# A planner that books busy intervals, earlier memory loads, and mLSTM scores from split float32r parts

## The chip, the cores and the metric

The kernel runs on one core of one Trainium2 chip. The metric is the device time of one execution in microseconds (us), the median of several runs. Engines are named as in the profile: PE multiplies matrices (PEld loads its weights), DVE is the vector engine, ACT the scalar engine, POOL the third elementwise engine, SP and POOL also issue transfers (DMA).

## The reference

The kernel computes a trunk of two layers on 512 tokens of width 1024, all in float32, with a memory of 256 rows. Cut to what matters:

```python
# layer 0: x += fox_diff_mixer(rms_norm(x)); x += cross_attention(x, mem); x += conv_ffn(x)
# layer 1: x += mlstm_mixer(rms_norm(x));    x += cross_attention(x, mem); x += conv_ffn(x)
# out = rms_norm(x)
def fox_diff_mixer(xn, ...):           # 8 forgetting heads (fq, fk, fv), 4 differential heads (dq, dk, dv)
    p = softmax(q @ k.T * scale + F_q - F_k)            # forgetting: decays F from a gate
    p = softmax(q1 @ k1.T * scale) - lam * softmax(q2 @ k2.T * scale)   # differential
    d_out = rms_norm(p @ v, subln) * (1 - lambda_init)  # a norm per head
    return concat(fox_out, d_out) @ w_out
def mlstm_chunkwise(q, k, v, i_pre, log_f):             # 4 heads; q, k after a causal convolution and silu
    scores = (q @ k.T) * W                              # W: exp of gate sums, masked
    num = scores @ v
    den = maximum(abs(scores.sum(-1)), exp(-m))
    h = num / den                                       # then a norm per head, an output gate, and @ w_out
```

## The kernel before

Everything is written transposed where PE needs it, in tiles of 128 partitions. Most products are "split": a float32 value is kept as a high part (a cast to float32r) and a low part (the rest, also float32r), and `mm3` (lines 340 to 342 before, 373 to 375 after) issues three float32r products: high x high, low x high, high x low. Weights come by SP into one of three `raw` buffers of 128 x 1024; ACT casts them to `wh`, DVE subtracts to `wl` (line 262 in the profile is the helper that records all DVE and ACT operations; it is line 295 after). The products gather in four accumulator banks `acc`, in two banks `s` and two banks `w` of PSUM.

Layer 0's mixer runs over heads. The differential heads come first: projections dv, dq, dk; q and k are rotated into `qa`, `ka`, `kb`; a score row (lines 750, 751; 783, 784 after) of up to 512 columns is reduced with its mask or decay on DVE into `x` and `sm`; the scaled row is turned (line 781; 814) by transposes through a `w` bank into `pt`; the weigh (lines 793 and 1008; 826 and 1041) multiplies `pt` with v. Each differential head and the first three mLSTM heads end in a "far norm" (`p_far_norm`): sums of squares on PE (line 499; 532), `z` on DVE, a power on POOL, the roots written to memory and read back spread over all partitions as `hrb` (lines 448 and 452; 481 and 485, both issued by POOL), and a DVE step that multiplies by them. The first stretches of the next weights' work (`p_fill`: the memory's keys `xk`, and the output projection `wo`) fill PE where the mixer itself has none.

Layer 1's mixer projects values (`mv`, token major), queries and keys (`mqk`) and output gates (`mog`). `conv` makes q and k; the gates' columns come by small transposes (line 1630; 1663). Per head come four scores, one for each block of 128 keys with 512, 384, 256 and 128 queries (line 1721), multiplied by a mask tile `mk` into `at`; the denominators (lines 1743, 1744; 1781 after) sum the four `at` with a matrix of ones; the numerators (line 1765; 1802) multiply `at` with v.

The order within the mixers and attentions is set by a planner, class `Plan`. Its items have a length on PE, dependencies, a priority, banks and buffers they take and free, and a chain of steps on ACT ("A"), DVE ("D"), POOL ("G") or waiting ("-") that follows. Where several are ready the lowest priority number goes first. Before, each engine is one number, the time from which it is free:

```python
            for e, d in pick.chain:
                u = max(u, eng[e]) + d
                eng[e] = u
```

The instructions are issued in the order in which items are picked, and on the chip each engine runs its own in that order. The FFN has another planner, class `Sched`.

Of the kernel before, what the change touches and what calls it, by code (L numbers as in the profile page):

```python
# [30 lines left out]
ROW_DMA, SPREAD_DMA, LATE = 2.7, 6.0, 12.0  # L31
# [51 lines left out]

class Plan:
# [3 lines left out]
    def __init__(self, prev=None, hold=(), **res):  # L88
        self.items = []
        self.t = prev.t if prev else 0.0  # L90
        self.eng = dict(prev.eng) if prev else {"A": 0.0, "D": 0.0, "G": 0.0}
        self.res = {k: [0.0] * n for k, n in res.items()}
        self.banks = {b: 0.0 for b in range(4) if b not in hold}
        self.res["acc"] = self.banks.values()

    def add(self, fn, dur=0.0, deps=(), prio=None, take=(), free=(), chain=(), pre=(), after=0.0, order=(), load=(), st=None):
        it = Item(fn, dur, [d for d in deps if d is not None], len(self.items) if prio is None else prio, take, free, chain, pre, after, order, load, st)
        it.n = len(self.items)
        self.items.append(it)
        return it  # L100

    def run(self):
        todo = sorted(self.items, key=lambda i: (i.prio, i.n))
        eng, t = self.eng, self.t
        while todo:
            soon, pick = float("inf"), None
            held = set()
            for i in todo:
                if any(d.ready is None for d in i.deps + i.order) or held & set(i.take):
                    continue  # L110
                held |= set(i.take)
                if any(len(self.res[r]) < i.take.count(r) for r in i.take):
                    continue
                at = max([i.after] + [d.ready for d in i.deps] + [sorted(self.res[r])[i.take.count(r) - 1] for r in i.take])
# [8 lines left out]
            todo.remove(pick)  # L123
            for r in pick.take:
                if r == "acc":
                    b = min(self.banks, key=self.banks.get)
                    del self.banks[b]
                    pick.st.setdefault("banks", []).append(b)
                else:
                    self.res[r].remove(min(self.res[r]))  # L130
            for e, d in pick.pre:
                eng[e] = max(eng[e], t - 4.0) + d
            t += pick.dur
            u = t + (0.1 if pick.chain else 0.0)
            for e, d in pick.chain:
                if e == "-":
                    u += d
                    continue
                u = max(u, eng[e]) + d
                eng[e] = u  # L140
                u += 0.06
            for e, d in pick.load:
                eng[e] = max(eng[e], t) + d
            pick.ready = u
            pick.fn()
            for r in pick.free:
                if r == "acc":
                    self.banks[pick.st["banks"].pop(0)] = u
                else:
                    self.res[r].append(u)  # L150
        self.t = t
        return t
# [136 lines left out]
class Builder:  # L289
# [64 lines left out]
    def p_proj(self, pl, src, xs, evac, chain, deps=(), kdeps=None, edeps=(), prio=None, n=SEQ, nk=KB8, order=None, etake=(), per=2, eorder=(), load=()):  # L354
# [5 lines left out]
        for c, e in zip(cuts, cuts[1:] + [nk]):  # L360
# [12 lines left out]
            for k in ks:  # L373
# [4 lines left out]
                pre=(("A", 0.12 * nk), ("D", 0.14 * nk)) if first else (), st=st,  # L378
# [1607 lines left out]
```

## Time and profile before

| what | value |
|---|---|
| median of 3 runs | 1425.7 us (1424.77 to 1426.21) |
| profiled execution, its own time | 1423.48 us |
| its span | 1421.7 us |
| mean granted PE clock | 0.998 |
| PE busy | 1403.3 us, 99% |
| DVE, ACT, POOL busy | 80%, 58%, 9% |
| layer 0: mixer, output projection and attention, FFN | 0 to 225, to 330, to 725 us |
| layer 1: mixer, output projection and attention, FFN | to 890, to 1090, to 1415 us |

The span runs from the first to the last instruction of the profiled execution; 1.8 us lie around it. Busy shares are averages over these stages. In rows of instructions, lines are those of the kernel before; a tile's name stands ahead of `<-`, its inputs behind.

### The profile page before, as it was taken

What the parts mean: (1) busy time and instruction counts of PE and PEld (TensorE: products, weight loads), DVE (VectorE), ACT (ScalarE), POOL (GpSimd) and SP (SyncE); (2) the same over time, 40 slices, a digit from 0 to 9 for tenths busy, and PEclk for the clock granted to TensorE, in tenths of its full rate; (3) what the DMA queues carried; (4) which work ended last, traced back from release to release, by engine and by line L of the source; (5) the groups of instructions that cost most, each with busy time, mean ns of one, the idle gap of its engine ahead of it and who ended that gap; (6) DMA issues with size and microseconds to landing.
All of it is one profiled execution on the core that took longest, in us unless ns stands there. A gap on an engine that the chain in (4) does not pass through costs nothing.

```text
span 1421.7 us, 22241 instructions
## 1 busy us (share of the span) xinstructions
PE 1403.3 (99%) x8440; PEld 1262.9 (89%) x8440; DVE 1133.5 (80%) x1906; ACT 823.8 (58%) x1382; POOL 129.9 (9%) x189
## 2 busy tenths in 40 slices
PE   9999999999999999999999999999999999999998
PEld 7878788899889999999887788989988999999997
DVE  7778596666689999999768657667667999999984
ACT  7777574444476656566456654445445665656655
POOL 0001240000001111110001210000000111111000
PEclk9999999999999999999999999999999999999999
DMA  5233224323248777773233322323323886777522
GB/s 205 90 108 108 90 79 152 132 76 133 86 150 217 191 180 184 182 182 106 86 105 112 105 95 97 119 92 120 130 74 120 212 202 171 193 179 185 143 77 80
DMA packets 69211, 190.02 MB, mean 134 GB/s; under 512 B 7552, under 2 KB 7552, under 8 KB 69104
## 3 DMA queue, kind: packets, MB, share of 16 engines
q1 hardware_dynamic: 55648, 153.48, 32.3%
q0 software_dynamic: 12448, 34.00, 13.7%
q8 instruction: 66, 1.08, 0.3%
q10 hardware_dynamic: 1008, 1.12, 0.2%
q14 instruction: 41, 0.34, 0.1%
HBM read 186.43 MB, written 2.15 MB: 133 GB/s over the span
## 4 chain that ended last, share of the span: by engine, by line
PE 83%; DVE 8%; ACT 4%; issue 3%; DMA 1%; POOL 1%; SPq 0%; POOLq 0%; DVEq 0%; ACTq 0%
PE acc L340 16%; PE acc L341 16%; PE acc L342 16%; PE w L340 5%; PE w L342 5%; PE w L341 5%; PE s L340 3%; PE s L341 3%; PE s L342 3%; PE acc L402 2%; PE acc L404 2%; PE acc L403 2%; DVE wl L262 2%; DVE x L262 1%; PE w L1765 1%
## 5 line engine op out<-in xcount | busy, mean ns | idle before, releaser
L262 ACT CAST wh<-raw 128x1024 fp32r<-128x1024 f32 (+2 forms) x229 | 235.0, 1027 | 205.6 <-PE acc L341 118.8
L262 DVE TENSOR_TENSOR wl<-raw,wh 128x1024 fp32r<-128x1024 f32 (+2 forms) x229 | 274.2, 1198 | 38.7 <-ACT wh L262 38.2
L340 PE MATMUL acc<-xh,wh 128*128 128x512 f32 (+1 forms) x800 | 278.6, 348 | 0.8 <-ACT v L262 0.8
L341 PE MATMUL acc<-xl,wh 128*128 128x512 f32 (+1 forms) x800 | 274.0, 343 | 0.0
L342 PE MATMUL acc<-xh,wl 128*128 128x512 f32 (+1 forms) x800 | 273.6, 342 | 0.0
L340 PEld LDWEIGHTS acc<-xh,wh 128*128 128x128 f32 x800 | 152.5, 191 | 14.5 <-ACT v L262 1.2
L342 PEld LDWEIGHTS acc<-xh,wl 128*128 128x128 f32 x800 | 152.4, 190 | 13.9
L341 PEld LDWEIGHTS acc<-xl,wh 128*128 128x128 f32 x800 | 152.5, 191 | 13.2
L262 DVE SCALAR_TENSOR_TENSOR c<-hs,vec,c 128x512 f32<-128x512 f32 x176 | 131.8, 749 | 3.8 <-ACT c L262 0.8
L340 PE MATMUL w<-ah,wh 128*128 128x512 f32 x304 | 115.7, 381 | 0.2 <-ACT c L262 0.2
L342 PE MATMUL w<-ah,wl 128*128 128x512 f32 x304 | 115.2, 379 | 0.0
L341 PE MATMUL w<-al,wh 128*128 128x512 f32 x304 | 115.2, 379 | 0.0
L262 ACT ACTIVATE c<-hs,vec 128x512 f32<-128x512 f32 x88 | 70.8, 811 | 9.9 <-DVE hs L262 5.4
L262 ACT CAST ah<-c 128x512 fp32r<-128x512 f32 x44 | 27.2, 619 | 83.8 <-DVE c L262 83.8
L262 DVE TENSOR_TENSOR x<-acc,x 128x512 f32<-128x512 f32 (+1 forms) x43 | 28.1, 653 | 54.2 <-PE acc L342 53.4
L340 PEld LDWEIGHTS w<-ah,wh 128*128 128x128 f32 x304 | 57.6, 190 | 8.0 <-DVE x L262 0.9
L342 PEld LDWEIGHTS w<-ah,wl 128*128 128x128 f32 x304 | 57.5, 189 | 8.1
L341 PEld LDWEIGHTS w<-al,wh 128*128 128x128 f32 x304 | 57.6, 190 | 6.5
L342 PE MATMUL acc<-mem,wl 128*128 128x256 f32 (+1 forms) x192 | 59.9, 312 | 0.0
L340 PE MATMUL acc<-mem,wh 128*128 128x256 f32 (+1 forms) x192 | 59.6, 311 | 0.0
L341 PE MATMUL acc<-mem,wh 128*128 128x256 f32 (+1 forms) x192 | 59.6, 311 | 0.0
L1446 POOL DMA_DIRECT2D sa<-in_up_dram x36 | 30.8, 857 | 290.6 <-DMA sa<-in_up_dram 212.7
(357 smaller groups left out, 3750.5 us busy)
## 6 DMA issues: line engine op xcount, KB each, us to landing
raw<-in_up_dram SPq DMA_DIRECT2D x52, 512.0 KB, 3.7
sa<-in_up_dram SPq DMA_DIRECT2D x36, 512.0 KB, 3.4
sa<-in_up_dram POOLq DMA_DIRECT2D x36, 512.0 KB, 5.9
raw<-in_down_dram SPq DMA_DIRECT2D x32, 512.0 KB, 3.6
ra<-in_up_dram SPq DMA_DIRECT2D x36, 256.0 KB, 4.0
sb<-in_up_dram POOLq DMA_DIRECT2D x36, 256.0 KB, 4.9
raw<-in_xk_dram SPq DMA_DIRECT2D x16, 512.0 KB, 3.2
raw<-in_wo_dram SPq DMA_DIRECT2D x16, 512.0 KB, 3.3
```

What stands on the lines that cost most here:

```text
L262: i = issue(*a, **k)
L340: mm(out, wh, xh, start=first, stop=False, skip_group_check=parts)
L341: mm(out, wh, xl, start=False, stop=False, skip_group_check=parts)
L342: mm(out, wl, xh, start=False, stop=last, skip_group_check=parts)
L402: mm(ps, xh[k][:, ts], wh, start=(k == 0), stop=False)
L403: mm(ps, xh[k][:, ts], wl, start=False, stop=False)
L404: mm(ps, xl[k][:, ts], wh, start=False, stop=(k == 7))
L1446: return add("POOL", 0.0029 * cols, lambda: nc.gpsimd.dma_start(out(), src(), accum_op=ALU.add), deps, due, (), (), 6.0)
L1765: nc.tensor.matmul(ps[:, lo:], vv[s][:, c], a[:], start=(s == 0), stop=(s == 3))
```

## The change

The planner. An engine is now a list of busy intervals, and a step goes into the first gap that holds it (`place`). An item that is ready only later than 2.5 us from now (`HOLD`) no longer keeps its banks from items of lower priority. The plan is first made as a whole (`ordered`) and then issued. A projection's accumulator bank counts as free after the first step of its chain (`soon`). Costs of steps are changed (a cast 0.5 to 0.6, the roots on POOL 1.05 to 1.3, the far norm's round trip `LATE` 12 to 15). Memory loads are issued 16 us ahead of their use instead of 10. In layer 1 the gates' chain is one wait of 14 us with its load beside it.

The mLSTM. q and k are kept as high and low parts (one more DVE step each), and a score is an `mm3` instead of one float32 product. The denominators' sum is completed by a copy, split by a cast on ACT and a subtraction on DVE, and multiplied with ones in two float32r products of 512 columns, instead of float32 products of 128 and 384. The sum uses a tile of tag `th` instead of `mk`. In all PE's rows go from 8101 to 8133, DVE's from 1809 to 1825, ACT's from 1275 to 1278; POOL and SP keep theirs.

```diff
-ROW_DMA, SPREAD_DMA, LATE = 2.7, 6.0, 12.0
+ROW_DMA, SPREAD_DMA, LATE = 2.7, 6.0, 15.0
...
+HOLD = 2.5
...
-        self.eng = dict(prev.eng) if prev else {"A": 0.0, "D": 0.0, "G": 0.0}
+        self.eng = prev.eng if prev else {"A": [], "D": [], "G": []}
...
+        def place(e, at, d):
+            b = eng[e]
+            while b and b[0][1] < t - 8.0:
+                b.pop(0)
+            n = 0
+            for n, (x, y) in enumerate(b):
+                if at + d <= x:
+                    break
+                at = max(at, y)
+            else:
+                n = len(b)
+            b.insert(n, (at, at + d))
+            return at + d
...
-                held |= set(i.take)
-                if any(len(self.res[r]) < i.take.count(r) for r in i.take):
+                if any(len(res[r]) < i.take.count(r) for r in i.take):
+                    held |= set(i.take)
                     continue
...
+                if at < t + HOLD:
+                    held |= set(i.take)
...
             for e, d in pick.pre:
-                eng[e] = max(eng[e], t - 4.0) + d
+                place(e, t - 4.0, d)
...
             for e, d in pick.chain:
-                if e == "-":
-                    u += d
-                    continue
-                u = max(u, eng[e]) + d
-                eng[e] = u
-                u += 0.06
+                u = u + d if e == "-" else place(e, u, d) + 0.1
+                clear = clear or u
...
-            last = pl.add(lambda c=c: load(c), 0, (), 0, after=at + step * c - 10.0, order=[*order, last])
+            last = pl.add(lambda c=c: load(c), 0, (), 0, after=at + step * c - 16.0, order=[*order, last])
...
-            g = pl.add(lambda: None, 0, [g], 1, chain=(("A", 1.0), ("D", 7.0), ("A", 0.5)))
-            gk = pl.add(lambda: None, 0, [g], 2, chain=(("-", ROW_DMA),))
+            g = pl.add(lambda: None, 0, [g], 1, chain=(("-", 14.0),), load=(("A", 5.0), ("D", 7.0)))
+            gk = pl.add(lambda: None, 0, [g], 2, chain=(("-", 4.0),), load=(("A", 2.4), ("D", 1.2)))
...
-                out = self.til(mp, tag, bufs=2)
-                nc.scalar.activation(out[:], c[:], AF.Copy, scale=scale)
-                return out
+                hi, lo = (self.til(mp, tag + i, dtype=F32R)[:] for i in ("", "l"))
+                nc.scalar.activation(hi, c[:], AF.Copy, scale=scale)
+                nc.vector.scalar_tensor_tensor(out=lo, in0=c[:], scalar=scale, in1=hi.bitcast(F32), op0=ALU.mult, op1=ALU.subtract)
+                return hi, lo
...
-                        nc.tensor.matmul(ps[:, :n], st["k"][:, ks], st["q"][:, lo:512], start=True, stop=True)
+                        (kh, kl), (qh, ql) = st["k"], st["q"]
+                        self.mm3(ps[:, :n], kh[:, ks], kl[:, ks], qh[:, lo:], ql[:, lo:], True, True)
...
-                    asum = st["sum"] = self.til(mp, "mk")
+                    asum = st["sum"] = self.til(mp, "th")
...
+                    nc.vector.tensor_copy(asum[:, :P], at[0][0][:, :P])
+                    st["d"] = [self.til(mp, "mk", dtype=F32R)[:] for _ in range(2)]
+                    self.split(*st["d"], asum[:])
...
-                    nc.tensor.matmul(den[:, :P], self.ones[:], st["at"][0][0][:, :P], start=True, stop=True)
-                    nc.tensor.matmul(den[:, P:], self.ones[:], asum[:, P:], start=True, stop=True)
+                    for i, part in enumerate(st["d"]):
+                        nc.tensor.matmul(banked(den[:]), self.onesr[:], alternate(part), start=i == 0, stop=i == 1)
```

More of the change, by code (lines that the diff above doesn't have):

```diff
@@ L377, in p_proj, with p_proj_tok @@
                 fn, 3 * len(ks) * MM * n / 512, d, prio, take=("acc", "wt") if first else (), free=("wt",) if e == nk else (),
[L378 removed]
+                pre=(("A", 0.13 * nk), ("D", 0.14 * nk)) if first else (), st=st,
             )
[L380 to L382 removed]
+        return pl.add(lambda: evac(st["ps"]), 0, [last, *edeps], prio, take=etake, free=("acc",), chain=chain, order=eorder, load=load, st=st, soon=True)
+    def p_proj_tok(self, pl, src, xs, ntok, evac, deps=(), kdeps=None, edeps=(), prio=None, n=512, etake=(), ready=None, rest=True):
         st = {}
```

129 lines of the change are left out of this document (71 added, 58 removed).

## The prediction

> **What bounds the kernel now.** First the page: busy shares and the chain that ended last.
>
> ```profile
> span 1421.7 us, 22241 instructions
> PE 1403.3 (99%) x8440; PEld 1262.9 (89%) x8440; DVE 1133.5 (80%) x1906; ACT 823.8 (58%) x1382; POOL 129.9 (9%) x189
> PE 83%; DVE 8%; ACT 4%; issue 3%; DMA 1%; POOL 1%; SPq 0%; POOLq 0%; DVEq 0%; ACTq 0%
> ```
>
> PE is the bound, so the time changes in two ways only: PE gets less work, or waits less. Next the stages, in the windows view (columns: window, its length, busy us of PE, PEld, DVE, ACT and POOL, granted clock, DMA share, GB/s).
>
> ```profile
> 20.00:150.00 130.00, 127.37 (x633) 109.18 (x632) 99.94 (x260) 99.00 (x198) 12.42 (x19) 1.00 0.32 104
> 150.00:156.00 6.00, 3.50 (x22) 3.18 (x21) 3.85 (x12) 2.40 (x7) 3.23 (x5) 0.94 0.33 87
> 156.00:160.00 4.00, 4.00 (x13) 3.23 (x13) 2.58 (x5) 2.64 (x6) 1.96 (x4) 0.66 0.24 66
> 180.00:210.00 30.00, 28.55 (x208) 24.39 (x208) 28.80 (x102) 22.91 (x59) 12.03 (x22) 1.00 0.19 63
> 330.00:725.00 395.00, 394.84 (x2602) 366.76 (x2602) 347.54 (x512) 229.67 (x368) 33.64 (x42) 1.00 0.56 152
> 725.00:890.00 165.00, 161.43 (x739) 133.44 (x738) 112.68 (x172) 91.41 (x134) 24.17 (x41) 1.00 0.31 101
> ```
>
> Layer 0's mixer ends near 225; after the attention the FFN fills 330 to 725, and layer 1's mixer, the mLSTM, ends near 890. The FFN is full, and the change doesn't touch it. What can be won lies in the two mixers. The waits view puts a few names on it (who waits, for whom; us in total, times, longest).
>
> ```profile
> PE w L781 <- DVE pt L262: 2.5, 1, 2.5
> PE s L1721 <- ACT k L262: 1.8, 2, 0.9
> PE s L1630 <- DVE cv L262: 1.5, 1, 1.5
> PE w L793 <- ACT pt L262: 1.0, 1, 1.0
> PE w L781 <- DVE sm L262: 0.9, 1, 0.9
> ```
>
> Records of matmuls overlap (0.38 us long, 0.22 apart), so their idle time understates what is lost. I therefore count work from start to start. These rows give the steps (start, length):
>
> ```profile
> 198.97 0.33 PE L751 MATMUL s<-kb,qa 128*128 128x384 f32 x1
> 199.13 0.38 PE L750 MATMUL s<-ka,qa 128*128 128x512 f32 x1
> 199.34 0.38 PE L751 MATMUL s<-kb,qa 128*128 128x512 f32 x1
> ...
> 162.50 0.27 PE L750 MATMUL s<-ka,qa 128*128 128x256 f32 x1
> 162.61 0.28 PE L751 MATMUL s<-kb,qa 128*128 128x256 f32 x1
> ...
> 787.94 0.38 PE L1743 MATMUL w<-at,ones 128*128 128x128 f32 x2
> 788.16 0.81 PE L1744 MATMUL w<-mk,ones 128*128 128x384 f32 x2
> 788.81 0.82 PE L1721 MATMUL s<-q,k 128*128 128x256 f32 x4
> ...
> 160.88 0.49 PE L781 MATMUL w<-ident,x 128*128 128x128 f32 x3
> 161.12 0.46 PE L340 MATMUL acc<-xh,wh 128*128 128x512 f32 x1
> ```
>
> A float32r product takes 0.16 us for 384 columns, 0.21 to 0.22 for 512, 0.11 for 256. A plain float32 one (recorded as two) takes 0.22 for 128 and 0.65 for 384: 1.7 ns a column. Three transposes take 0.24. With these steps, 180 to 210 holds 23.7 us of work and loses 6.3, at a DVE that is busy 28.8 of 30 us; 160 to 225 loses 9.1 in all, 20 to 150 6.1, 725 to 890 4.8.
>
> **The products.** Per head the mLSTM's scores are four float32 products of 512, 384, 256 and 128 columns, 1280 x 1.7 = 2.17 us, and the denominators 512 columns, 0.87. After: scores 3 x (0.22 + 0.16 + 0.11 + x), denominators two float32r products of 512, 0.44. x, a float32r product of 128 columns, is not in the trace. Between 0.08 (a transpose of 128 columns above) and 0.22 (float32) I take 0.11, the nearest row of that type. A head saves 3.04 - 1.80 - 0.44 = 0.80, four heads **3.2 us** (1.9 to 3.6). By the Trainium skill, TensorE: Matmul & The Clock Gate, section "Wait — 56ns, not 53.3ns?", x would be 0.056 on a warm array; the saving would be estimated at 3.8.
>
> On DVE this adds eight low parts, four subtractions and four copies; on ACT four casts. From the groups by line (busy us, mean ns; then idle time before and its releasers), the nearest operations:
>
> ```profile
> L262 DVE SCALAR_TENSOR_TENSOR cv<-hs,vec,cv 128x512 f32<-128x512 f32 x24 | 18.3, 763 | 0.3
> L262 DVE COPY pt<-w 128x128 f32<-128x128 f32 x24 | 6.9, 286 | 2.1 <-ACT pt L262 1.7 <-PE w L781 0.2
> L262 DVE COPY pt<-w 128x384 f32<-128x384 f32 x12 | 6.5, 548 | 0.9 <-PE w L781 0.9
> ```
>
> That is 8 x 0.76, four subtractions at no more than that and 4 x 0.29, some 10 us on a DVE busy 112.7 of 165. It is hidden unless it stands in front of a wait.
>
> **The far norm of 150 to 160.** The chain view, then timeline rows of DVE and PE:
>
> ```profile
> 145.80 0.61 POOL roots L448
> 146.41 2.03 issue
> 148.46 3.71 DMA hrb<-roots
> ...
> 152.19 0.75 DVE L262 SCALAR_TENSOR_TENSOR ta<-ta,warm,hrb 128x512 f32<-128x512 f32 x1 [2.06 <-DMA hrb<-roots]
> ...
> 155.26 0.69 PE L781 MATMUL w<-ident,x 128*128 128x128 f32 x2 [2.50 <-DVE pt L262]
> ...
> 156.59 0.63 PE L340 MATMUL acc<-xh,wh 128*128 128x512 f32 x1
> ...
> 158.72 0.38 PE L342 MATMUL acc<-xh,wl 128*128 128x512 f32 x1
> ```
>
> The norm's roots go through memory twice; DVE reaches the step that needs them too soon, stands 2.06 us, and the turn's copy behind it keeps PE idle for 2.50. Then PE runs at half speed: 0.43 a matmul instead of 0.22 for the five from 156.59 to 158.72 (1.07 us), and 1.33 instead of 0.57 for the two transposes and two products before (0.76). Price 4.3 us.
>
> The Trainium skill, same page, section "HAM oscillation — how this bites in real kernels", wants idle gaps under about 3.4 us. This one of 2.5 already cost the clock (0.66 granted in 156 to 160), so the measurement decides; by the rule the gap alone would be priced, 2.5.
>
> DVE, layer 0, from behind that norm's z to the waiting step; before:
>
> ```order
> L262 TENSOR_TENSOR wl_1738<-raw_1736,wh_1737 128x1024
> L262 COPY pt_1116<-w_1489 128x128
> L262 ISA x_140,sm_1507<-s_1500,tb_1501 128x384
> L262 ISA sm_1507 128x1
> L262 TENSOR_TENSOR kb_115<-tmp_1509,ka_298_1511 64x512
> L262 TENSOR_TENSOR kb_117<-tmp_1509,ka_299_1515 64x512
> L262 RECIPROCAL sm_1507<-sm_1507 128x1
> L262 TENSOR_SCALAR x_140<-x_140,sm_1507 128x384
> L262 COPY pt_1370<-w_1543 128x128
> L262 ISA x_142,sm_1557<-s_1550,tb_1551 128x384
> L262 ISA sm_1557 128x1
> L262 SCALAR_TENSOR_TENSOR ta_1421<-ta_1421,warm,hrb_1568 128x512
> ```
>
> After, the norm with the least room in that stage (two z stand together, then):
>
> ```order
> L295 TENSOR_SCALAR z_1302<-s_1297 128x4
> L295 COPY pt_1013<-w_1281 128x128
> L295 SCALAR_TENSOR_TENSOR tmp_1322<-acc_244_1263,rb_335 128x512
> L295 TENSOR_TENSOR wl_1424<-raw_1422,wh_1423 128x1024
> L295 TENSOR_TENSOR qa_256_1324<-tmp_1322,qa_256_1324 64x512
> L295 TENSOR_TENSOR qa_257_1327<-tmp_1322,qa_257_1327 64x512
> L295 TENSOR_TENSOR tmp_1367<-acc_261_1336,rb_335 128x512
> L295 TENSOR_TENSOR wl_1532<-raw_1530,wh_1531 128x1024
> L295 TENSOR_TENSOR kb_114<-tmp_1367,ka_266_1369 64x512
> L295 SCALAR_TENSOR_TENSOR ta_1241<-ta_1241,warm,hrb_1351 128x512
> ```
>
> The step now stands behind the evacuation of acc_261, which PE ends 36 matmuls of 512 columns (7.8 us) after the sums, and behind three more DVE steps, some 10.5 us in all, against 8.9 us from z (143.30) to 152.19. PE first needs what is queued behind it after 66 such matmuls, 14 us. The wait goes: **-4.3 us** (bounds 0 and -4.9, with the small waits around it).
>
> **The rest of layer 0's mixer.** In 20 to 150, the waits view above has a transpose that waits 0.9 for a score row and a weigh that waits 1.0 for a copy. The first rotary scores show a third (timeline, PE):
>
> ```profile
> 131.23 0.27 PE L750 MATMUL s<-ka,qa 128*128 128x256 f32 x1
> ...
> 132.57 0.38 PE L340 MATMUL acc<-xh,wh 128*128 128x512 f32 x1
> ```
>
> Between the two stand four products of 256 columns: 1.34 us instead of 0.45, so 0.9 is lost to the rotated keys. In the new order each of the three users has more PE work between itself and its producer (the rotary scores 30 matmuls of 512 columns, 6.5 us, where they had 3.9 to 4.2 and came 0.9 late), so 2.8 go. New is a denser stretch of scores at about 45 to 60, where copies, score rows and evacuations share DVE: I put 1 us there (0 to 2.5). Net **-1.8** (-2.8 to -0.3).
>
> 160 to 225 is the least certain term. The filler is now the first three output projections instead of the memory keys, and six transposes stand in a row near its end. PE before:
>
> ```order
> L781 MATMUL w_2393<-ident,x_138 128x128 x4
> L781 MATMUL w_2400<-ident,x_141 128x128 x4
> L342 MATMUL acc_518_2489<-mh_128,wl_2485 128x512
> L340 MATMUL acc_518_2489<-mh_129,wh_2484 128x512
> L341 MATMUL acc_518_2489<-ml_135,wh_2484 128x512
> L1008 MATMUL w_2425<-pt_2109,v_1207 64x512
> ```
>
> and after:
>
> ```order
> L814 MATMUL w_2374<-ident,x_142 128x128 x3
> L814 MATMUL w_2380<-ident,x_138 128x128 x3
> L814 MATMUL w_2385<-ident,x_141 128x128 x4
> L814 MATMUL w_2392<-ident,x_137 128x128 x4
> L1041 MATMUL w_2399<-pt_2143,v_1228 64x512
> ```
>
> The filler between turns and weigh is gone. Two w banks serve six turns, so each waits for the copy of the turn two before it (0.29 to 0.55 us by the groups above, against 0.15 to 0.2 of transposes between): some 0.3 for four of them, 1.2. The weigh then waits for the last copies, 0.8. The output projection follows the last weigh directly and needs its evacuation, a cast on ACT and a subtraction on DVE (about 1.3 against 0.4 of covering work): 0.9. The keys' weights behind it come another 0.6 late. That makes 3.5 at this end. Ahead of it 180 to 210 lost 6.3; by the order most turns and scores there now have more projection matmuls between producer and user, and I leave 2 us of waits. 9.1 becomes 5.5 or so: **-3.5** (0 to -6).
>
> **Layer 1's mixer.** Its waits now:
>
> ```profile
> 748.83 0.38 PE L404 MATMUL acc<-wh,xl 128*128 128x512 f32 x1
> 750.68 0.38 PE L1630 MATMUL s<-ident,cv 4*128 4x4 f32 x4 [1.47 <-DVE cv L262]
> ...
> 769.44 0.38 PE L342 MATMUL acc<-xh,wl 128*128 128x512 f32 x1
> 770.75 1.77 PE L1721 MATMUL s<-q,k 128*128 128x512 f32 x4 [0.94 <-ACT k L262]
> ```
>
> The gate columns' transposes wait 1.6 (1.85 between starts less 0.22); they move 42 matmuls later, to the end of the next projection, and that wait goes. The scores wait 1.1 and, at 784, 1.0 for k. PE there, before:
>
> ```order
> L341 MATMUL acc_1538_8231<-xl_1436_7733,wh_8226 128x512
> L342 MATMUL acc_1538_8231<-xh_1435_7732,wl_8227 128x512
> L1721 MATMUL s_8249<-q_8123,k_8167 128x512
> L1721 MATMUL s_8258<-q_8123,k_8167 128x384
> L340 MATMUL acc_1538_8231<-xh_1441_7763,wh_8226 128x512
> ```
>
> and after:
>
> ```order
> L374 MATMUL acc_1541_8237<-xl_1446_7792,wh_8232 128x512
> L375 MATMUL acc_1541_8237<-xh_1445_7791,wl_8233 128x512
> L373 MATMUL s_8261<-q_8116,k_8169 128x512
> L374 MATMUL s_8261<-ql_8117,k_8169 128x512
> L375 MATMUL s_8261<-q_8116,kl_8170 128x512
> L373 MATMUL s_8272<-q_8116,k_8169 128x384
> ```
>
> 18 matmuls (3.9 us) instead of 12 (2.6) now stand between k's projection and its score. k took 2.6 + 1.1 = 3.7, so it just fits; the new low part kl takes 0.76 more but is read two products later. I leave 1.2 us for both heads, and 1.4 for the other new steps (the denominators wait for a cast and a subtraction at 881, selects on POOL). 4.8 becomes 2.6: **-2.2** (+0.5 to -3.5).
>
> **The sum.** -3.2 - 4.3 - 1.8 - 3.5 - 2.2 = -15.0. Against the profiled execution (1423.5: span 1421.7 and 1.8 around it) this gives 1408.5; that run lies 2.2 below the median of 1425.7, to which I apply it: **1410.7 us**.
>
> **The rivals.** (a) The planner brings nothing: each wait removed comes back elsewhere, since DVE's work in layer 0 is the same. Only the products' 3.2 remain: 1422.5. For it speaks DVE's 28.8 of 30 us; against it that the roots' wait is a matter of order, not of DVE's work. (b) Slower: the engines' queues run in order, while the planner fills gaps in intervals. If DVE on the chip falls behind the plan, the stretch 20 to 150 becomes like 180 to 210, which loses 6.3 / 30 = 0.21 us per us against its own 6.1 / 130 = 0.05. Over 90 us that is +14.7; with -3.2 and -4.3 it gives +7.2, 1432.9. It decides from 46 us on (0.16 x 46 = 7.5). Against it: DVE is busy 99.9 of 130 there and gets no work. (c) All waits of the two mixers' ends go, -22: 1403.7; against it the six turns in a row.
>
> **How the numbers follow.** Forecast 0.62, (a) 0.15, (b) 0.10, (c) 0.13. A measurement of this kernel tells 0.2% (2.9 us) from no change. (a) lies on that bound and counts half as faster, half as the same, and a little of the forecast's upper end joins it: faster 0.80, same 0.09, slower 0.11. The range reaches over (c) and (a): 1402.5 to 1423.5; it leaves out (b).
>
> **What would show it.** Right: no DVE wait on hrb above 0.5 us and a clock of 1.00 in every stage up to 330; the first waits of PE in layer 0 at the last weighs near 190 to 200; gate transposes without a wait; three products of about 0.22 each for the first score. Wrong: DVE busy above 0.95 over 60 us of 20 to 150; score waits on kl above 1 us per head; a 128-column product that takes 0.2.

## The result, and the profile after

The changed kernel takes 1430.3 us (median of 7 runs, 1428.34 to 1431.30), the kernel before 1424.8 in the same session (7 runs): a ratio of 1.0035, 95% interval 1.0026 to 1.0044. The forecast was 1410.7 with a range to 1423.5. The change makes this kernel slower by 0.35%, and the forecast is wrong in sign. The profiled execution of after took 1428.6 us.

The page of the changed kernel: span, busy time of each engine, and the shares of the chain that ended last.

```profile
span 1426.8 us, 22271 instructions
PE 1404.5 (98%) x8448; PEld 1263.2 (89%) x8448; DVE 1139.0 (80%) x1922; ACT 827.1 (58%) x1386; POOL 129.7 (9%) x189
PE 83%; DVE 7%; ACT 6%; DMA 2%; issue 1%; POOL 0%; SPq 0%; POOLq 0%; DVEq 0%; ACTq 0%
```

PE is still the bound, so the 5.1 us that the span grew are work or idle time of PE. The windows view of after, with the columns of the prediction:

```profile
20.00:150.00 130.00, 127.21 (x633) 108.86 (x632) 98.81 (x264) 97.49 (x199) 14.17 (x24) 1.00 0.32 102
150.00:156.00 6.00, 6.00 (x29) 4.79 (x28) 5.87 (x15) 4.96 (x11) 0.26 (x1) 1.00 0.26 102
156.00:160.00 4.00, 4.00 (x26) 3.53 (x25) 3.31 (x8) 2.50 (x5) 0.29 (x1) 1.00 0.56 150
180.00:210.00 30.00, 28.46 (x160) 21.06 (x159) 23.63 (x86) 17.93 (x50) 8.56 (x17) 1.00 0.15 45
725.00:890.00 165.00, 157.98 (x729) 132.92 (x728) 119.47 (x188) 92.51 (x135) 24.33 (x41) 0.98 0.32 101
```

The stall of 150 to 156 is gone (PE 6.00 of 6.00 instead of 3.50, clock 1.00 in 156 to 160 instead of 0.66). Layer 1's mixer went the other way: PE 157.98 of 165 instead of 161.43, and a clock of 0.98. PE's waits say on whom it waits:

```profile
PE s L373 <- ACT k L295: 5.2, 2, 3.0
PE s L783 <- DVE sm L295: 1.9, 2, 1.6
PE s L783 <- ACT memrb L295: 1.4, 1, 1.4
PE s L373 <- DVE at L295: 1.3, 1, 1.3
PE acc L375 <- DVE wl L295: 1.1, 1, 1.1
```

Of before's five the transposes' 2.5 on `pt` and the gates' 1.5 on `cv` are gone; the scores' wait for k has grown from 1.8 to 5.2, scores that wait for a row's reduction (`sm`) had 0.9, and the other three entries are new. Counted from start to start as in the prediction (each matmul's distance to the next one, less its step), PE's work fell from 1380.9 to 1377.8 us, and this was lost:

| us | before | after | predicted change | measured change |
|---|---|---|---|---|
| PE's work (the products) | 1380.9 | 1377.8 | -3.2 | -3.1 |
| 150 to 160 (the far norm) | 4.5 | 0.2 | -4.3 | -4.2 |
| 20 to 150 | 6.1 | 6.5 | -1.8 | +0.4 |
| 160 to 225 | 9.1 | 12.6 | -3.5 | +3.5 |
| 725 to 890 | 4.8 | 12.5 | -2.2 | +7.7 |
| elsewhere | 9.0 | 9.9 | 0 | +0.9 |

Two terms came out to a tenth or so. Most of the rest is three places.

**First place: the first score of layer 1.** DVE's timeline, before (first row) and after (second): the step that writes the second gate row. Then PE's timeline of after.

```profile
754.53 0.69 DVE L262 TENSOR_TENSOR rows<-num,sqt 4x512 fp32r<-4x512 f32 x1
...
755.39 0.68 DVE L295 TENSOR_TENSOR rows<-num,sqt 4x512 fp32r<-4x512 f32 x1
```

```profile
759.05 0.41 PE L1663 MATMUL s<-ident,cv 4*128 4x4 f32 x4
...
770.07 0.38 PE L375 MATMUL acc<-xh,wl 128*128 128x512 f32 x1
772.72 0.48 PE L373 MATMUL s<-q,k 128*128 128x512 f32 x1 [2.27 <-ACT k L295]
...
774.33 0.63 PE L373 MATMUL acc<-xh,wh 128*128 128x512 f32 x1
774.76 0.63 PE L374 MATMUL acc<-xl,wh 128*128 128x512 f32 x1
```

The gate transposes no longer wait, as predicted. But the first score waits 2.4 us for k (772.72 - 770.07 - 0.22) instead of 1.1, and behind it PE runs at half speed (774.33 to 774.76: 0.43 a matmul). 765 to 780 loses 4.5 instead of 1.2: 2.4 in the wait, 1.6 at half speed (it lasts from 774.17 to 777.58), and 0.5 in the products between the two.

**Second place: the third head's norm.** DVE and PE of after:

```profile
860.79 0.74 DVE L295 SCALAR_TENSOR_TENSOR cv<-hs,vec,cv 128x512 f32<-128x512 f32 x1
864.38 0.75 DVE L295 SCALAR_TENSOR_TENSOR num<-num,vec,hrb 128x512 f32<-128x512 f32 x1 [2.85 <-DMA hrb<-roots]
865.05 1.53 DVE L295 SCALAR_TENSOR_TENSOR cv<-hs,vec,cv 128x512 f32<-128x512 f32 x2
...
882.00 0.74 DVE L295 SCALAR_TENSOR_TENSOR num<-num,vec,hrb 128x512 f32<-128x512 f32 x1
```

```profile
871.65 0.38 PE L375 MATMUL acc<-xh,wl 128*128 128x512 f32 x1
875.00 0.48 PE L373 MATMUL s<-q,k 128*128 128x512 f32 x1 [2.98 <-ACT k L295]
```

DVE stands 2.85 us at a step that needs the norm's roots, in the middle of the convolution (`cv`) of the last head's q. Everything behind is late, and PE waits 3.1 us for that head's k. In the program a norm has two such steps in succession, one for each half of the head. The one at 882 is the first, in the place that the planner gave it; the one at 864 is the second, which the framework's scheduler moved up, 24 DVE steps ahead of its partner and before the roots were there. So the order of the plan is not kept for a step that nothing ties. 868 to 880 loses 5.2, of which 1.5 at half speed; before, nothing.

**Third place: the end of layer 0's mixer.** PE of after (x9: nine instructions in a row):

```profile
208.59 1.88 PE L814 MATMUL w<-ident,x 128*128 128x128 f32 x9
210.68 1.12 PE L814 MATMUL w<-ident,x 128*128 128x128 f32 x8 [0.21 <-DVE pt L295]
212.23 2.50 PE L1041 MATMUL w<-pt,v 128*64 128x512 f32 x16 [0.43 <-DVE pt L295]
215.41 0.92 PE L373 MATMUL acc<-qa,wh 128*128 128x512 f32 x3 [0.68 <-ACT qa L295]
...
219.35 0.38 PE L375 MATMUL acc<-mem,wl 128*128 128x256 f32 x1 [1.10 <-DVE wl L295]
```

Turns, weigh, output projection and keys follow with no filler between them. 205 to 225 loses 5.8 us; before, 2.8.

### The profile page after: what moved, and what is told of

It reads as the page before. It is cut to its first block, busy times and chain, and to the rows that moved or that the text cites. A ratio compares the mean times of both kernels' runs of the same rounds, so it can differ in the third digit from the quotient of the medians.

```text
span 1426.8 us, 22271 instructions
## 1 busy us (share of the span) xinstructions
PE 1404.5 (98%) x8448; PEld 1263.2 (89%) x8448; DVE 1139.0 (80%) x1922; ACT 827.1 (58%) x1386; POOL 129.7 (9%) x189
## 4 chain that ended last, share of the span: by engine, by line
PE 83%; DVE 7%; ACT 6%; DMA 2%; issue 1%; POOL 0%; SPq 0%; POOLq 0%; DVEq 0%; ACTq 0%
PE acc L373 17%; PE acc L374 16%; PE acc L375 16%; PE w L373 5%; PE w L375 5%; PE w L374 5%; PE s L375 3%; PE s L373 3%; PE s L374 3%; PE acc L435 2%; PE acc L436 2%; PE acc L437 2%; DVE wl L295 2%; DVE cv L295 1%; ACT wh L295 1%
## 5 line engine op out<-in xcount | busy, mean ns | idle before, releaser
L540 POOL TENSOR_TENSOR y<-z,power 128x4 f32<-128x4 f32 (+1 forms) x17 | 20.9, 1227 | 408.6 <-DVE z L295 408.6
```

What stands on the lines that cost most here:

```text
L540: nc.gpsimd.tensor_tensor(out=y, in0=z, in1=self.power[:, :nt], op=ALU.pow)
```

## The experiments

Times are medians; ratios are to the kernel before in the same session (1423.6 to 1424.7 us). "Lost" is counted as above, from one profile. Runs of one kernel spread over 2 to 7 us, so a difference of 1 us between two variants says little by itself, and the traces carry the argument.

### Is it the free step, the split, or layer 0's order?

**both_follow**: the changed kernel with the second step of each norm tied. `follow()` makes the next DVE instruction depend on the one issued just before it; `p_far_norm` ties the first step so, and nothing tied the second.

```diff
                     for d in range(2):
                         nm = st["num"][d]
+                        if d:
+                            nc.vector.follow()
                         nc.vector.scalar_tensor_tensor(out=nm[:], in0=nm[:], scalar=self.col("hn", 2 * h + d), in1=rb[:], op0=ALU.mult, op1=ALU.mult)
```

> The changed kernel, with both DVE steps that multiply by the spread roots of a head's norm tied behind the step issued before them (before, only the first of the two was tied; the other one was free to move up). In the trace after, the free one stands on DVE at 864.4 and waits 2.85 us for the roots; PE then waits 3.1 us for k at 871.7 and runs at half speed behind it. Theory roots: the score wait at 871 goes or falls below 0.5 us with its half speed: -4 to -5 us, about 1425.5. Theory split (the low parts crowd DVE): the roots' wait only takes the place of work that DVE has to do anyway, PE still waits 2 us or more there: -1 us or less, about 1429.5.

Measured 1426.4, ratio 1.0008 (0.9999 to 1.0018). Its trace:

```profile
855.57 1.41 DVE L295 SCALAR_TENSOR_TENSOR num<-num,vec,hrb 128x512 f32<-128x512 f32 x2
...
872.02 0.38 PE L375 MATMUL acc<-xh,wl 128*128 128x512 f32 x1
872.23 0.38 PE L373 MATMUL s<-q,k 128*128 128x512 f32 x1
```

Both steps stand together and nobody waits; the score follows the projection in 0.21. 868 to 880 loses 0.2 instead of 5.2. The second place is shown: it is the free step.

**no_lo**: the changed kernel without the low parts of q and k, and without their step in the planner's cost.

```diff
-                nc.vector.scalar_tensor_tensor(out=lo, in0=c[:], scalar=scale, in1=hi.bitcast(F32), op0=ALU.mult, op1=ALU.subtract)
-                return hi, lo
+                return hi, hi
...
-            cc = (("D", 0.6), ("A", 0.7), ("D", 2.3), ("A", 0.7), ("D", 0.66), ("A", 0.7), ("D", 0.66))
+            cc = (("D", 0.6), ("A", 0.7), ("D", 2.3), ("A", 0.7), ("D", 0.66), ("A", 0.7))
```

> The changed kernel without the eight DVE steps that make the low parts of q and k; the high part stands in for the low one in the products, so PE's work stays and the scores have only the high parts' precision. Theory split: DVE is crowded by them; the score waits at 770 (2.4 us) and 871 (3.1 us) fall below 1.5 each and no half speed follows: -4 to -6 us, about 1425. Theory roots: 0.7 us less at each of the two waits (one low part stands ahead of k in each), half speed behind 871 stays: -1.5 to -2.5, about 1428.3.

Measured 1427.1, ratio 1.0016 (1.0004 to 1.0027). The first score still waits 2.6 us (771.23); the place at 871 shrinks to 2.3. That does not clear the low parts: without their cost the planner puts 44 matmuls instead of 50 between the gate transposes and the first score, so PE comes 1.3 us sooner, k comes 1.1 us sooner, and the wait stays. What the low parts add is told by the distances under gate_late.

**planner_only**: the changed planner, costs and places, with float32 scores and denominators as before.

```diff
-                        self.mm3(ps[:, :n], kh[:, ks], kl[:, ks], qh[:, lo:], ql[:, lo:], True, True)
+                        nc.tensor.matmul(ps[:, :n], st["k"][:, ks], st["q"][:, lo:512], start=True, stop=True)
```

> The changed kernel with scores and denominators as float32 products of whole values, as before the change; planner and costs as after. The products cost 3.2 us more of PE. Theory split: without the low parts on DVE the waits for k at 770 and 871 and their half speed fall by 5 us or more together: 1428 to 1429. Theory roots or order: the planner's order alone makes these waits, they stay within 1 us: 1432.5 to 1433.5.

Measured 1429.9, ratio 1.0029 (1.0017 to 1.0040). 740 to 920 loses 10.7 (12.4 in after). The planner's changes alone cost the time; they do not need the split. Which of them, apart from HOLD (hold_all, below), no run separates: the intervals were not run with the old costs, nor the new costs with the old booking.

**old_mix0**: layer 0's mixer by the planner, helpers and costs of before, layer 1 as in after.

```diff
+        self.__class__ = Old
+        Old.mix0(self)
+        self.__class__ = Builder
```

> The changed kernel with layer 0's mixer planned as before: the old planner, its costs and lead times there, everything behind it as after. Layer 0's mixer lost 22.8 us before and 22.7 after, so if the stages are independent the time stays within 1 us, about 1430. If the new order of layer 0 shifts what follows (loads, the first attention), it moves by 2 us or more, either way.

Measured 1428.3, ratio 1.0018 (1.0007 to 1.0029). 0 to 240 loses 24.0 (after 22.7, before 22.8), and layer 1 still loses 13.5. Layer 1's loss doesn't come from layer 0.

### Can the three places be mended?

**conv_margin** (with the tie): the planner counts 3 us more from each projection of q and k to its scores.

```diff
-            cc = (("D", 0.6), ("A", 0.7), ("D", 2.3), ("A", 0.7), ("D", 0.66), ("A", 0.7), ("D", 0.66))
+            cc = (("D", 0.6), ("A", 0.7), ("D", 2.3), ("A", 0.7), ("D", 0.66), ("A", 0.7), ("D", 0.66), ("-", 3.0))
```

> The changed kernel with both steps of the third norm tied (as in both_follow) and one more edit: the planner's cost of the chain from k's projection to its score is 3 us longer, so that it puts six more matmuls of 512 columns (1.3 us) and what they displace between them. Theory 'chain cost': k takes 11.5 us where the planner counts some 7; the wait at about 770 of layer 1 (2.4 us, and 2.1 of half speed behind it in the changed kernel) goes or shrinks under 1 us; 740 to 920 loses 4 to 5 instead of 8.1, and the time is 1422 to 1424. Rival 'DVE is crowded there anyway': the wait moves to another score or gate of the same stretch, 740 to 920 still loses 7 to 9, and the time stays at 1426 to 1427.

Measured 1432.0, ratio 1.0049 (1.0031 to 1.0067): slower than either theory allowed. The first score waits only 0.28 idle. But then, on PE and DVE:

```profile
776.81 0.38 PE L374 MATMUL acc<-xl,wh 128*128 128x512 f32 x1
781.63 0.42 PE L373 MATMUL s<-q,k 128*128 128x256 f32 x1 [4.43 <-DVE at L295]
...
780.89 0.68 DVE L295 TENSOR_TENSOR at<-s,mk 128x512 f32<-128x512 f32 x1
```

Later scores came behind the next head's convolution in DVE's queue; the first evacuation `at` (the DVE step that empties a score's bank) runs 7 us behind its score, both `s` banks stay full, and the third score waits 4.6. A wait of 3.2 for `hsq` follows at 823; why was not followed up.

**hold_all**: the rule of before for what is not ready yet.

```diff
-HOLD = 2.5
+HOLD = 1e9
```

> The changed kernel with HOLD at 1e9: a piece of work that is not ready keeps back the resources it takes from all pieces of lower priority, as in the planner before. Theory: the loss of the last 17 us of layer 0's mixer (4.7 us in the changed kernel: six turns in a row, the weigh, the first output projection, the keys) comes from the filler being used up early; with the filler held back it goes to about 1, 0 to 240 loses 18 to 20 instead of 22.7, layer 1's mixer stays as it was within 2 us, and the time is 1426 to 1428. Rival: what is held back leaves waits in 160 to 210 instead (the planner's rule filled those), 0 to 240 loses 22 to 25, and the time is 1430 or more.

Measured 1426.3, ratio 1.0012 (1.0002 to 1.0023). 205 to 225 loses 1.7 instead of 5.8, 0 to 240 19.6 instead of 22.7, layer 1 13.1. The third place is shown: it is the filler, used up early because HOLD lets work of lower priority take banks that work not ready within 2.5 us will want.

**all3**: both edits above and the tie.

> The changed kernel with the three edits together: both steps of the third norm tied, the chain to the scores 3 us longer, HOLD at 1e9. If the three losses are separate, the gains add: -4 (871), -2 to -4 (770), -3 (end of layer 0), which gives 1419 to 1422, faster than the kernel before. If the waits stand for a DVE that has too little room, it stays at 1425 to 1428.

Measured 1425.1, ratio 1.0005 (0.9995 to 1.0016). 0 to 240 loses 19.5, but conv_margin's wait is there too (4.7 at 774). It did not add up.

**follow_hold**: the tie and HOLD alone.

> The changed kernel with the two edits that each helped by itself: both steps of the third norm tied to their place, and HOLD at 1e9. Each took about 4 us off; they lie 600 us apart. If they add, 0 to 240 loses 19.5, 740 to 920 8 to 9, and the time is 1421.5 to 1423.5, under the kernel before. If the waits of layer 1 take some back, as they did in all3, it is 1424 to 1426.

Measured 1422.4, ratio 0.9994 (0.9985 to 1.0003): the two gains add, as expected (0 to 240 loses 19.3, 740 to 920 8.5). Against the kernel before, the difference is within the noise.

### What sets the first score?

**gate_late**: the kernel *before*, with its gate transposes 24 matmuls later and nothing else moved on PE.

```diff
-            uc = pl.add(ucols, 0.4, [g], 2, take=("s",), free=("s",), chain=(("D", 0.1),))
+            uc = pl.add(lambda: None, 0, [g], 2, chain=(("-", 7.0),))
+            uc = pl.add(ucols, 0.4, [uc], 2, take=("s",), free=("s",), chain=(("D", 0.1),))
```

> The kernel before with one move alone: the gate columns' transposes of layer 1 stand 24 matmuls (5.2 us) later on PE, behind q's projection of the first head; nothing else changes its place on PE. The prediction's step: their wait (1.6 us) goes, so the time falls by 1.6 to about 1423. Rival 'one chain': the steps of DVE and ACT from the norm to the first score run without slack, so PE gets to the first score 1.6 us sooner and waits there 2.4 to 2.8 us for k instead of 1.1; the first score still starts 15.5 us after the second rows step of DVE has begun plus 0.7, the time stays within 1 us of before, or grows by 1 to 2 where half speed follows the longer gap.

Measured 1424.6 against 1423.6, ratio 1.0007 (0.9998 to 1.0016). The gates' wait (1.6) is gone from the trace and the time did not fall. DVE and PE:

```profile
752.50 0.69 DVE L262 TENSOR_TENSOR rows<-num,sqt 4x512 fp32r<-4x512 f32 x1
...
765.89 0.38 PE L342 MATMUL acc<-xh,wl 128*128 128x512 f32 x1
768.11 1.77 PE L1722 MATMUL s<-q,k 128*128 128x512 f32 x4 [1.84 <-ACT k L262]
```

PE comes earlier and waits 2.0 for k instead of 1.1, and 1.9 instead of 1.0 at the next head's. From the second gate row to the first score it is 15.6 us here (one convolution step of 0.6 also moved ahead on DVE). The same distance is 16.22 in before (754.53 to 770.75), 16.21 in planner_only, 16.23 in no_lo, and 17.33 in after, both_follow and follow_hold, which have the low parts, whatever PE does meanwhile. (It is 17.9 in conv_margin and all3; the 0.6 more there was not followed up.) It is a chain of DVE and ACT. PE's order only decides where along it PE stands idle.

**one_tap**: the changed kernel with one tap step instead of three for the first head's q and k.

```diff
-                for tap in (2, 1, 0):
+                for tap in (2, 1, 0)[: 1 if blk in (0, 4) else 3]:
```

> The changed kernel with two of the three tap steps left out in the convolution of the first head's q and of its k in layer 1 (its result is not the reference's there): four DVE steps of 0.67 us less between the gate's rows and the first score, the planner's costs and PE's order as they were. 'One chain' of DVE and ACT: the first score starts 2 to 2.7 us sooner, its wait of 2.4 and the half speed behind it (2.1) go, and the time falls by 3.5 to 4.5, to about 1426, unless the wait for the evacuation at 794 grows. Rival 'PE or a transfer sets it': the wait stays above 1.5 us and the time within 1.5 us of the changed kernel.

Measured 1428.5, ratio 1.0037 (1.0024 to 1.0050), no better than after. The wait goes (score at 770.37, 765 to 780 loses 1.4 instead of 4.5), as 'one chain' has it; but 780 to 800 loses 3.8 instead of 1.5: a score waits 1.87 instead of 1.29 for the evacuations `at`, and half speed follows. The half of the expectation that named a time failed: the next place took most of it.

### What did the split cost in the old order?

**split_only**: before, with the split products alone (the diff of planner_only the other way round, and the denominators).

> The kernel before with the split scores and denominators alone, its planner and its costs unchanged. By the prediction's first term PE has 3.1 us less work; if nothing new waits, the time is 1421 to 1422. By the rival that DVE's eight low parts come in front of waits in any order, layer 1's mixer loses 7 or more instead of 5.1 and the time is 1424 to 1427.

Measured 1426.7, ratio 1.0013 (1.0001 to 1.0024): PE has 3.1 us less work and the kernel is slower. 740 to 920 loses 10.0 instead of 5.1.

**split_no_lo**: split_only without the low parts of q and k (the edit of no_lo, the planner's cost included, so the order changes too).

> The kernel before with the split products and its old planner, but without the two low parts of q and k in each head: each product with a low part takes the high part in its place, so PE has the same matmuls (the result is not the reference's). DVE has eight steps of 0.69 us less than in split_only. If these steps are what takes back the products' 3.1 us, 740 to 920 loses 5 to 6 instead of 10.0 and the time is 1421 to 1423. If it is the other new steps (casts, copies, the denominators' parts) or the changed places of the scores, it loses 8 to 10 and the time is 1425 to 1427.

Measured 1436.8, ratio 1.0094 (1.0080 to 1.0108): eight DVE steps *fewer*, and 10 us *slower*. No theory had that. DVE's waits at the roots in 725 to 890, split_only first, then split_no_lo, then after (us in total, times, longest):

```profile
DVE num L262 <- DMA hrb<-roots: 9.2, 3, 4.4
...
DVE num L262 <- DMA hrb<-roots: 14.7, 3, 7.5
...
DVE num L295 <- DMA hrb<-roots: 10.2, 2, 7.3
```

In before it is 2.9. Two of the three waits of split_no_lo are at a free step that landed elsewhere: 7.5 at 834 and 3.1 at 877, each over 19 us ahead of its partner. The third is not. The two steps of the first head's norm stand in their place, and the first of them waits 4.1:

```profile
817.74 0.75 DVE L262 SCALAR_TENSOR_TENSOR num<-num,vec,hrb 128x512 f32<-128x512 f32 x1 [4.11 <-DMA hrb<-roots]
...
819.07 0.75 DVE L262 SCALAR_TENSOR_TENSOR num<-num,vec,hrb 128x512 f32<-128x512 f32 x1
```

PE's longest waits there, 5.3 at 818 and 3.3 at 879, come right behind this one and behind the free step at 877.60. Some 7 of the 10 us are half speed, by an estimate from the mean granted clock of all its runs (0.993, split_only 0.998). This kernel was not run with the tie, so what the free step costs it stays open. Three kernels add the tie (the edit of both_follow) to kernels that have the step free:

**split_follow**:

> split_only (the kernel before with the split products, its planner unchanged) with both steps of each far norm of layer 1 tied to their place on DVE. Theory 'the free step': what took back the products' 3.1 us there is DVE standing at the roots (9.2 us in three waits) where the scheduler put the free second step too early; the waits at 813 and 877 (1.7 each) go, 740 to 920 loses 5 to 7 instead of 10.0, and the time is 1420.5 to 1422.5. Rival: the low parts on DVE cost it in any order; 740 to 920 loses 9 to 10 and the time stays at 1425 to 1427.

Measured 1423.9, ratio 0.9996 (0.9987 to 1.0004). DVE waits 1.6 at roots instead of 9.2, the wait at 877 is gone, and 740 to 920 loses 8.1: between the two theories. 3.0 more than in before_follow is left: 2.6 at 800 to 815 (1.7 of it one numerator that waits for ACT's `hsq`, the denominators' evacuation, which now comes behind a cast and a subtraction) and 1.4 at the output projection (908), less 1.0 elsewhere. These are read from the trace; no run takes them apart.

**planner_follow**:

> planner_only (the changed planner and costs, old products) with both steps of each far norm of layer 1 tied. 'The free step': the wait at 812 (2.5, and half speed behind it) and that at 877 (1.1) go, 740 to 920 loses 5 to 7 instead of 10.7, and the time is 1424 to 1426. Then the planner's order in layer 1 is no better and no worse than the old one, and what is left over against the kernel before is layer 0's end. Rival: the order itself is worse there; 740 to 920 loses 9 or more, the time stays at 1428 to 1430.

Measured 1428.1, ratio 1.0026 (1.0016 to 1.0035). 740 to 920 loses 6.7 instead of 10.7, as the free step has it, but 1.7 of these 4.0 are one stretch at half speed fewer in this profile. The median fell by 1.8 and the ratio by 0.0003, inside the intervals: the time that was expected did not come. What is left over against before in this profile is 1.6 us here, 0.5 in layer 0's mixer, and 2.4 in waits of the FFN (445, 1136), which come and go between the profiles of most kernels here; how much of these stays in the median is open.

**before_follow**:

> The kernel before with both steps of each far norm of layer 1 tied. Its DVE stands at the roots for 2.9 us in two waits that PE does not feel (740 to 920 loses 5.1, at the gates and the first head). By 'the free step' that is luck of this order: nothing to gain, the time is 1423 to 1424.5, within 0.1% of before. If it falls by over 2 us, the tie gains by something else than the waits at the roots.

Measured 1424.3, ratio 0.9996 (0.9987 to 1.0004), 740 to 920 loses 5.1: nothing to gain, as expected.

**fh_m15**: follow_hold with 1.5 us more in the first head's chain.

```diff
-                ke = self.p_proj(pl, t["mqk"][4 + h], ..., cc, edeps=[norm], prio=p, eorder=[qe])
+                ke = self.p_proj(pl, t["mqk"][4 + h], ..., cc + ((("-", 1.5),) if h == 0 else ()), edeps=[norm], prio=p, eorder=[qe])
```

> follow_hold with 1.5 us more in the planner's cost of the first head's chain from k's projection to its score, in that head alone: six more matmuls (1.3 us) stand ahead of the first score, and 12 instead of 6 + 6 between the second and the third. By 'one chain' the first score starts where it did; its wait falls from 2.4 to 1.1 and the half speed behind it (2.1 us) goes: 740 to 920 loses 5 to 6 instead of 8.5, and the time is 1419 to 1420.5, 0.2 to 0.3% under the kernel before. Rival, as in conv_margin: the evacuations of the scores fall behind the next head's convolution on DVE and the third score waits over 2 us; the time is 1422 to 1426.

Measured 1420.2 (5 runs), ratio 0.9969 (0.9957 to 0.9981): faster than both kernels. The first score, and layer 1's mixer in the windows:

```profile
768.90 0.48 PE L373 MATMUL s<-q,k 128*128 128x512 f32 x1 [0.97 <-ACT k L295]
...
725.00:890.00 165.00, 160.82 (x772) 135.50 (x771) 120.56 (x190) 95.36 (x140) 25.05 (x41) 1.00 0.32 100
```

The score starts 17.33 after the second gate row (751.57), as in after; six more matmuls stand ahead of it, so it waits 1.1, and no half speed follows (clock 1.00). 740 to 920 loses 6.4, a little over what was expected: a wait of 2.1 for `at` is left at 788.

## Why the prediction was wrong

**The products** were right: -3.1 of PE's work (-3.2 predicted). Two of the 128-column products, not in the trace before, take 0.18 us from start to start:

```profile
881.14 0.22 PE L373 MATMUL s<-q,k 128*128 128x128 f32 x1
881.20 0.28 PE L374 MATMUL s<-ql,k 128*128 128x128 f32 x1
881.32 0.28 PE L375 MATMUL s<-q,kl 128*128 128x128 f32 x1
```

That is 0.09 each where 0.11 was taken. The Trainium skill's figure for it (TensorE: Matmul & The Clock Gate, "Wait — 56ns, not 53.3ns?"), 0.056, is met by the first of these steps and not by the second. What failed is the step from work to time: split_follow and before_follow have the same ratio, 0.9996, so in the old order the split gains nothing that these runs can tell (each interval reaches 1.2 us to either side). "It is hidden unless it stands in front of a wait" named the condition and did not look for the wait. By the trace of split_follow it is the denominators' cast and subtraction, ahead of `hsq`, and the output projection. The low parts lengthen the chain to the first score by 1.1 us, but six more matmuls stand ahead of it there, and 740 to 800 loses no more than in before_follow.

**The far norm of 150 to 160** was right: the DVE step of `hrb` runs at 150.14 without a wait, and the 4.3 us are gone. The 1.8 of the price that were half speed were luck of the one profile: before_follow and gate_late have the same order there and waits of 2.6 and 2.3, and kept a clock of 1.00.

**20 to 150** failed: +0.4 instead of -1.8. The weigh's wait (1.0) and the loss at the first rotary scores (0.9) went, as predicted. The third wait that was to go, a transpose's 0.9 for a score row, was misread: it stands at 193.90, in the next stretch (first row, before). New is a wait of 1.61 at the rotary scores of the next row (after), and smaller ones around it.

```profile
193.90 0.63 PE L781 MATMUL w<-ident,x 128*128 128x128 f32 x4 [0.93 <-DVE sm L262]
...
136.92 0.27 PE L783 MATMUL s<-ka,qa 128*128 128x256 f32 x1
...
141.73 0.38 PE L783 MATMUL s<-ka,qa 128*128 128x256 f32 x1 [1.61 <-DVE sm L295]
```

By DVE's rows it takes up the score row that 141.73 waits for behind two steps on `qa`, and ACT's casts of `qa` stand behind squares and scalings of the memory, which the change loads 6 us earlier. The early loads alone do not make this wait: hold_all keeps them, and there the same scores, at 131.85, wait 0.36. A kernel with the old load time was not run.

**160 to 225** failed in its middle step, "I leave 2 us of waits" for 180 to 210: 180 to 210 loses 6.6 where it lost 6.3, 1.5 of it at a new wait, for the memory's norm (`memrb`) at 183.68. The end, priced at 3.5, came out at 5.8 in 205 to 225. The fillers that "most turns and scores there now have" were the ones that the end then lacked. hold_all shows it.

**Layer 1** failed three times, +7.7 instead of -2.2.
- "That wait goes" of the gates: it went, and came back at the first score. The wait was priced where PE stood, not by what it waited for. gate_late does this one move to the kernel before and gains nothing.
- "k took 2.6 + 1.1 = 3.7, so it just fits": this measured k from PE's side, with the 12 matmuls that stood there. k's time is set by DVE, whose queue then held the gate rows, q's convolution and a weight's low part; with PE 1.6 earlier, k takes as much longer. The low part that was counted, kl, comes only at 772.70, when the first score has its k. Not counted was q's, ql, which stands on DVE ahead of k's convolution (row below); with the low parts the chain is 17.33 long instead of 16.22. So k takes 6.3 us (18 matmuls and a wait of 2.4) instead of 3.7, and 1.6 + 1.1 make up that difference. And the gap of 2.4 brought half speed, 1.6 us more, which the same prediction had priced at 156 and left out here.

```profile
766.08 0.69 DVE L295 SCALAR_TENSOR_TENSOR ql<-cv,q 128x512 fp32r<-128x512 f32 x1
```

- The free step at 864 was not in the sum. Before, DVE waited at roots for 2.9 us in this stage too, and PE did not feel it; that was taken as room, where it was luck.

**Rival (b)** named the mechanism, "the engines' queues run in order, while the planner fills gaps in intervals", with 0.10, but put it in 20 to 150, where DVE is busy 98.8 of 130 us. That its 1432.9 lies near the measured 1430.3 is luck. What was measured fits it best in 760 to 790, the first head's convolutions, where DVE is busy 28.0 of 30 us (25.6 before):

```profile
760.00:790.00 30.00, 27.70 (x124) 23.64 (x123) 27.98 (x45) 17.43 (x29) 4.67 (x11) 0.94 0.37 122
```

## What to carry to other kernels

A wait that a new order removes is only gained if what it waited for is also earlier: follow the releaser back until its engine has idle time, and if the distance between two of its steps is the same in every version (16.2 us here, 17.3 with the low parts), the wait will move and not go. Where a step waits for a long transfer on an engine that runs in order, tie every instruction that reads the transfer, not just the first; one left free lands where any unrelated edit puts it. And where a queue is full, a margin in the planner's costs helps at that one place only: 1.5 us for one head gained 2 us, 3 us for all heads lost about 3 to 6.

## What the runs showed of the clock

Behind a wait PE ran at full or at half speed, and the length of the wait alone does not tell which. The windows view of after, with a wait of 1.61 us idle ahead of 141.73, and of both_follow, which has the same matmuls there in the same order and waited 1.42:

```profile
139.29:142.70 3.41, 1.80 (x10) 1.31 (x9) 3.31 (x10) 2.22 (x7) 0.94 (x2) 1.00 0.47 153
142.70:146.11 3.41, 3.08 (x15) 2.46 (x14) 3.27 (x16) 2.44 (x9) 1.98 (x4) 1.00 0.01 4
```

```profile
140.05:143.46 3.41, 1.66 (x10) 1.23 (x10) 3.35 (x15) 1.54 (x6) 1.22 (x3) 1.00 0.44 156
143.46:146.87 3.41, 3.41 (x10) 2.92 (x10) 2.68 (x9) 2.62 (x9) 2.49 (x5) 0.50 0.00 0
```

In all 18 profiles a spell at half speed, apart from the kernel's start and end, lasts 3.41 us, or two or three times that. Within a profile the edges of the spells lie whole multiples of 3.41 us apart, wherever the waits lie, and the windows above are cut on that grid of their run. What goes with the clock is PE's idle time summed over one such stretch: 1.61 us in after's, 1.75 in both_follow's (1.42 and a second wait of 0.33). Of the stretches at full speed in the 18 profiles, all 20 with over 1.9 us idle were followed by half speed, 5 of the 9 between 1.75 and 1.9, and none of the others. A long wait that an edge cuts in two can so cost no clock: the 2.6 of before_follow at 154 did not, the 2.5 of before, in the same order, did.

Where the first edge lies changes from run to run (4.0 to 7.0 us after the span's start), so a wait of some 2 us should be priced with and without half speed, up to 1.7 us a stretch. By the mean granted clocks of the runs, 0.9964 in after and 0.998 in the kernel before, about 2 of the 5.5 us between them are half speed; this is an estimate. The Trainium skill (TensorE: Matmul & The Clock Gate, "What's actually happening") says that the gate watches a free-running window of 3.4 us and goes back after an idle one. The first half fits these rows; the second does not, since a stretch with 1.75 of its 3.41 us idle was enough.
